# Eight gate blocks in seven-product pairs, and the SSD output product beside attention, on one core of Trainium2

## The chip, the cores and the metric

The kernel runs on one core of one Trainium2 chip. The metric is the device time of one execution in microseconds (us), from the median of several runs; lower is better.

## The reference

One decoder block on a sequence of 1024 tokens and 1024 channels, all in float32. Cut to what matters here:

```python
h = rms_norm(x, pre_norm1_w) * (1.0 + sc1) + sh1
proj = h @ w_in
z, xbc, dt_raw, q, k, v, gates = split(proj)
y_ssd = ssd_branch(z, xbc, dt_raw, ...)                 # (1024, 1024), before its output product
y_att = diff_attention_branch(q, k, v, ...)             # 8 heads, each with two softmaxes
gate_ssd, gate_att = split(sigmoid(gates), 2)           # 1024 channels each
merged = gate_ssd * (y_ssd @ w_ssd_o) + gate_att * (y_att @ w_attn_o)
mix = merged @ w_out
x = x + g1 * rms_norm(mix, post_norm1_w)
# then a gated conv-FFN on x
```

## The kernel before

**Products.** Each float32 product is made of three matmuls, with both sides split into a high and a low part (`split`: ACT copies the high part, DVE subtracts to get the low part). A "block" is 128 output channels by all 1024 tokens. It needs 8 slices of the contraction, two halves of 512 tokens and three matmuls each: 48 matmuls of 128x512. Two blocks can also be made as a pair in seven products instead of eight (Strassen's scheme in Winograd's form, on halves of the contraction and of the tokens): 84 matmuls instead of 96, with extra sums of weights on DVE and extra sums of results on ACT and DVE. The sums of the token side (`HX`) are made once and serve all pairs.

**Order of the stages.** After the first norm:

1. Four SSD gate blocks (0 to 3) as plain blocks; the first is begun with the norm.
2. The loop over `pairs`: SSD gate blocks 4 to 7, one q/k pair, ten convolution blocks. While pair m runs, `post` finishes pair m-1. In the second and third pair the first sums of `w_ada` (`ada_sum`) run too.
3. The z, dt and v products and the SSD recurrence by chunks. At its end y lies in DRAM (`yd`), tokens by channels.
4. The q/k blocks 0 and 1: the list `seq` names the blocks in order, `fetch_seq` loads a block's weights two blocks ahead, `split_seq` splits them one block ahead. Between the halves of a block, `turn_y` turns columns of y: TensorE transposes four 128x128 pieces of `yr` (loaded from `yd`, one token half at a time by `load_y`), ACT and DVE make the high and the low part in `yT`, which stays in SBUF. The result of a q/k block gets its rotation in `rope` (ACT copy to `qf`, DVE `stream_shuffle` to `sw`, POOL and DVE products, a DVE sum, then `split` into `thhi`, `thlo`), and `store_qk` sends it to DRAM in 16 DMAs of 64 KB, high and low parts in turn.
5. The SSD output product: eight blocks of `w_ssd_o` on `yT`, each multiplied by its gate (`gsd`, DVE) and stored in `msd`.
6. Attention, head by head, eight blocks of 128 queries each. Its scores, transposes and value products leave TensorE waiting for softmax, so plain blocks fill in: `dense_stream` is a generator that gives three matmuls per step, and `fill(n)` takes n steps. It runs 18 blocks: q/k blocks 3 to 7 and the eight attention gate blocks `ga`. Work for ACT and DVE beside it (splits of weights, low parts, norms) stands in the queue `bg`, from which `run_bg` takes steps. `load_heads` loads q and k (`qst`, `kst`, `klo`) and v (`vt`) of the next head; the q and k of head 0 are loaded during stage 5.
7. The attention output product, merged with `msd` and the attention gate `gad`, and the rest of the layer.

**Order on the engines.** In stages 2 to 5 TensorE, DVE, ACT and SP (the queue that issues the DMAs) follow the program's order. In stage 6 TensorE, DVE, ACT and POOL do, and SP is ordered by the scheduler. SBUF is cut into 43 slots of 4 KB per partition (`SL`), given out first in, first out. `ps_wa` gives two PSUM banks in turn, `ps_wb` and `ps_wc` one each.

## Time and profile before

| | |
|---|---|
| Median of 3 runs | 1892.37 us (1890.81 to 1895.33) |
| Span of the profiled execution | 1889.7 us |
| TensorE busy | 1859.7 us, 98% |
| VectorE (DVE) busy | 1298.1 us, 69% |
| ScalarE (ACT) busy | 882.8 us, 47% |
| GpSimd (POOL) busy | 146.1 us, 8% |
| Mean granted TensorE clock | 0.994 |
| DMA | 322.09 MB, 170 GB/s over the span |

The profiled execution's own time is its span, which runs from the first to the last instruction. Lines of the trace have the source line, the engine, the result and the operands by the program's names, the number of instructions (x) and their times. "Idle before, <- releaser" is the time that the engine stood before an instruction, and what it waited for.

### The profile page before, as it was taken

What the parts mean: (1) busy time and instruction counts of PE and PEld (TensorE: products, weight loads), DVE (VectorE), ACT (ScalarE), POOL (GpSimd) and SP (SyncE); (2) the same over time, 40 slices, a digit from 0 to 9 for tenths busy, and PEclk for the clock granted to TensorE, in tenths of its full rate; (3) what the DMA queues carried; (4) which work ended last, traced back from release to release, by engine and by line L of the source; (5) the groups of instructions that cost most, each with busy time, mean ns of one, the idle gap of its engine ahead of it and who ended that gap; (6) DMA issues with size and microseconds to landing.
All of it is one profiled execution on the core that took longest, in us unless ns stands there. A gap on an engine that the chain in (4) does not pass through costs nothing.

```text
span 1889.7 us, 24926 instructions
## 1 busy us (share of the span) xinstructions
PE 1859.7 (98%) x9224; PEld 1561.0 (83%) x9224; DVE 1298.1 (69%) x1983; ACT 882.8 (47%) x1715; POOL 146.1 (8%) x139
## 2 busy tenths in 40 slices
PE   8999999999999999999999999999999999999998
PEld 8888889987888888888888788887878888888886
DVE  3677777689755237767667465377888888876545
ACT  4543542355543126565656323465554545465532
POOL 0000000045522000000000010000000000000001
PEclk8999999999999999999999999999999999999999
DMA  7447256678737746666542756022333322368744
GB/s 283 136 149 250 95 172 210 210 253 311 258 125 175 230 165 164 164 194 167 159 135 97 238 201 218 39 85 99 113 106 111 106 101 95 117 222 306 249 150 159
DMA packets 131898, 322.09 MB, mean 170 GB/s; under 512 B 17216, under 2 KB 41152, under 8 KB 131776
## 3 DMA queue, kind: packets, MB, share of 16 engines
q1 hardware_dynamic: 130464, 317.30, 51.5%
q0 software_dynamic: 1312, 3.19, 0.5%
q8 instruction: 73, 1.20, 0.3%
q14 instruction: 49, 0.40, 0.1%
HBM read 225.26 MB, written 95.17 MB: 170 GB/s over the span
## 4 chain that ended last, share of the span: by engine, by line
PE 82%; DVE 8%; ACT 4%; DMA 3%; issue 2%; SPq 0%; POOL 0%; POOLq 0%; ACTq 0%; DVEq 0%
PE upx L1772 3%; PE upx L1771 3%; PE upx L1773 3%; PE o L1463 3%; PE dx L2135 2%; PE dx L2136 2%; PE dx L2134 2%; PE dy L2136 2%; PE dy L2134 2%; PE dy L2135 2%; PE z L117 2%; PE z L118 2%; PE so L116 2%; PE ao L118 2%; PE ao L117 2%
## 5 line engine op out<-in xcount | busy, mean ns | idle before, releaser
L1771 PE MATMUL upx<-t,wu_t 128*128 128x512 f32 x264 | 103.6, 392 | 2.3 <-ACT evs L2191 1.6
L1772 PE MATMUL upx<-t,wu_t 128*128 128x512 f32 x264 | 103.0, 390 | 0.2 <-DVE t L1889 0.2
L1773 PE MATMUL upx<-t,wu_t 128*128 128x512 f32 x264 | 102.9, 390 | 0.0
L1745 ACT ACTIVATE wu_t<-sab 128x512 fp32r<-128x512 f32 x57 | 34.1, 627 | 129.8 <-DVE sab L1762 129.8
L1451 ACT COPY aT<-at 128x512 f32<-128x512 f32 (+2 forms) x96 | 46.1, 480 | 103.1 <-PE at L1450 103.1
L1463 PEld LDWEIGHTS o<-vt,aT 128*128 128x128 f32 x576 | 74.6, 191 | 9.8 <-ACT aT L1451 5.8
L95 DVE TENSOR_TENSOR g_lo<-gst,g_hi 128x1024 fp32r<-128x1024 f32 (+1 forms) x42 | 47.5, 1135 | 49.8 <-ACT g_hi L94 49.7
L1463 PE MATMUL o<-vt,aT 128*128 128x128 f32 x576 | 81.0, 277 | 0.3
L94 ACT ACTIVATE g_hi<-gst 128x1024 fp32r<-128x1024 f32 (+1 forms) x42 | 41.3, 987 | 64.7 <-DMA gst<-gld_s 35.7
L1424 DVE TENSOR_REDUCE nmx<-sc 128x1 f32<-128x640 f32 (+3 forms) x64 | 65.6, 1024 | 2.2
L1404 PE MATMUL sc<-kst,qst 128*128 128x512 f32 (+2 forms) x192 | 63.9, 341 | 0.0
L1405 PE MATMUL sc<-klo,qst 128*128 128x512 f32 (+2 forms) x192 | 63.2, 346 | 0.0
L1771 PEld LDWEIGHTS upx<-t,wu_t 128*128 128x128 f32 x264 | 49.6, 188 | 14.6 <-ACT evs L2191 2.0
L1789 DVE SCALAR_TENSOR_TENSOR ug<-cg,vec,ug 128x1023 f32<-128x1023 f32 (+1 forms) x44 | 56.3, 1280 | 6.8 <-ACT ug L1788 5.9
L1772 PEld LDWEIGHTS upx<-t,wu_t 128*128 128x128 f32 x264 | 49.6, 188 | 10.6 <-DVE t L1889 0.5
L1773 PEld LDWEIGHTS upx<-t,wu_t 128*128 128x128 f32 x264 | 49.6, 188 | 10.3
L1749 DVE TENSOR_TENSOR wu_t<-sab,wu_t 128x512 fp32r<-128x512 f32 x57 | 39.3, 690 | 26.5 <-ACT wu_t L1745 26.5
L1789 DVE SCALAR_TENSOR_TENSOR uv<-cv,vec,uv 128x1023 f32<-128x1023 f32 (+1 forms) x44 | 56.2, 1278 | 0.9 <-ACT uv L1788 0.9
L1440 DVE RECIPROCAL rsm<-ssum 128x2 f32<-128x2 f32 x64 | 10.6, 165 | 63.9 <-ACT p L1437 36.4
L1450 PE MATMUL at<-ident,p 128*128 128x128 f32 x288 | 47.8, 275 | 6.7 <-DVE p L1442 5.2
L143 POOL TENSOR_TENSOR rsf<-rsf,nhalf 128x1 f32<-128x1 f32 x8 | 5.6, 703 | 627.8 <-DVE rsf L142 625.1
L1442 DVE SCALAR_TENSOR_TENSOR p<-p,coef,p 128x128 f32<-128x128 f32 (+3 forms) x64 | 52.4, 818 | 2.2
(536 smaller groups left out, 5994.4 us busy)
## 6 DMA issues: line engine op xcount, KB each, us to landing
adas<-in_w_ada SPq DMA_DIRECT2D x32, 512.0 KB, 4.9
wdr<-in_w_down SPq DMA_DIRECT2D x22, 512.0 KB, 6.3
wtd<-wds SPq DMA_DIRECT2D x22, 512.0 KB, 4.8
wuf<-in_w_up SPq DMA_DIRECT2D x22, 512.0 KB, 3.5
gld_s<-gsum SPq DMA_DIRECT2D x22, 512.0 KB, 2.8
gst<-gld_s SPq DMA_DIRECT2D x20, 512.0 KB, 4.4
wdt_raw<-wtd SPq DMA_DIRECT2D x20, 512.0 KB, 4.9
wuv<-in_w_up SPq DMA_DIRECT2D x19, 512.0 KB, 3.5
```

Source lines behind the costliest of these rows:

```text
L117: T.matmul(ps, lh, rl, start=False, stop=False)
L118: T.matmul(ps, ll, rh, start=False, stop=(i == n - 1))
L1404: T.matmul(sc[:, n0:n1], qs_[s][:, tsl], ks_[s][:, n0:n1], start=True, stop=False)
L1424: V.reduce_max(nmx[:, bq, s : s + 1], sc[:, :L], axis=AX.X, negate=True)
L1463: T.matmul(po_of[j, grp][:, qi, :], at[:, k, :], vt[j % 2][:, kt, :], start=(kt == 0), stop=(kt == i))
L1771: T.matmul(out_, wh, xh_, start=(k == 0 and first), stop=False, skip_group_check=not first)
L1772: T.matmul(out_, wh, xl_, start=False, stop=False, skip_group_check=not first)
L1773: T.matmul(out_, wl, xh_, start=False, stop=(k == end), skip_group_check=not first)
L1789: V.scalar_tensor_tensor(u[:, d:], c_[:, : S - d], fw[:, 2 - d : 3 - d], u[:, d:], op0=ALU.mult, op1=ALU.add)
L2134: T.matmul(o, gh[:, kk, tsl], wh, start=(k == 0 and not more), stop=False, skip_group_check=more)
L2135: T.matmul(o, gh[:, kk, tsl], wl, start=False, stop=False, skip_group_check=more)
L2136: T.matmul(o, gl[:, kk, tsl], wh, start=False, stop=(k == KF - 1), skip_group_check=more)
```

## The change

The eight attention gate blocks leave attention and become four more pairs in the loop of stage 2. The SSD output product takes their place among the blocks that fill attention. Since y's columns would need sixteen slots until then, `turn_y` stores each in DRAM (`ytd`, 0.5 MB per column and token half), and each half is loaded back into the slots of `hT` as soon as the last q/k block has used that half; the last two q/k blocks and the first two SSD blocks are ordered by halves for this. The gate product of the SSD blocks goes to POOL (two operations per half, after a copy from PSUM by ACT). Stage 5 is gone. The weights of the first two attention blocks (`w_q3`, `w_k3`) are the fifth and sixth in `seq`; the rotation of the block `w_k` 1 becomes background work at the start of attention, ahead of the other steps in `bg`; head 0's q and k are loaded at the end of the third block of stage 4.

```diff
-    pairs = [("gs", 4, 5), ("gs", 6, 7), ("qk", 2, 2)] + [("xbc", b, b + 1) for b in range(2, 12, 2)]
+    pairs = [("gs", b, b + 1) for b in range(4, 16, 2)] + [("qk", 2, 2)] + [("xbc", b, b + 1) for b in range(2, 12, 2)]
...
-                SP.dma_start(gsd[b], c_)
+                SP.dma_start((gsd + gad)[b], c_)
...
-    seq = [("w_q", 0), ("w_k", 0), ("w_q", 1), ("w_k", 1)] + [("w_ssd_o", j) for j in range(8)]
+    seq = [("w_q", 0), ("w_k", 0), ("w_q", 1), ("w_k", 1), ("w_q", 3), ("w_k", 3)]
...
     def turn_y(k, half):
-        yT[k][half] = new_hl(f"yT{k}_{half}")
+        y_ = new_hl(f"yt{k}_{half}")
...
+        A.activation(y_[:, 0, :], ps, AF.Copy, scale=nw)
+        V.scalar_tensor_tensor(y_[:, 1, :], ps, nw, y_[:, 0, :].bitcast(F32), op0=ALU.mult, op1=ALU.subtract)
+        SP.dma_start(ytd[k][half], y_.bitcast(F32))
+        SL.put(y_)
...
+    def rope_steps(kind, b, ps):
+        return [
+            lambda: A.activation(qf, ps.rearrange("p h t -> p (h t)"), AF.Copy, scale=qscale[kind]),
+            lambda: (V.stream_shuffle(sw, qf, perm), G.tensor_tensor(qf, qf, ropc, op=ALU.mult)),
+            lambda: V.tensor_tensor(sw, sw, rops, op=ALU.mult),
+            lambda: V.tensor_tensor(qf, qf, sw, op=ALU.add),
+            lambda: split(th_hi, th_lo, qf),
+        ]
...
+            if n == 2:
+                qst, kst, klo = [[[SL.get(f"{x_}0_{s}", F32R) for s in range(2)]] for x_ in ("qst", "kst", "klo")]
+                for s in range(2):
+                    load_qk(s, qst[0][s], kst[0][s], klo[0][s])
...
-        for j in range(8):
...
-            block_half(ps[:, 0, :], seq_w[j + 4], yT, 0)
...
-                V.scalar_tensor_tensor(mout[:, hsl], gth[:, hsl], 1.0, ps[:, half, :], op0=ALU.add, op1=ALU.mult)
...
-    blocks = [(kind, b) for b in (3, 4, 5) for kind in ("w_q", "w_k")] + [("ga", 0)]
-    blocks += [(kind, b) for b in (6, 7) for kind in ("w_q", "w_k")] + [("ga", g) for g in range(1, 8)]
+    NQK = 10
+    blocks = [(kind, b) for b in range(3, 8) for kind in ("w_q", "w_k")] + [("so", j) for j in range(8)]
+    units = []
+    for n in range(len(blocks)):
+        units += [(n, 0), (n, 1)] if n not in (8, 9, 10, 11) else [(n // 2 * 2, n % 2), (n // 2 * 2 + 1, n % 2)]
...
+    def load_yT(half):
+        for k in range(KD):
+            SL.put(hT[k][half])
+            yT[k][half] = SL.get_last(f"yT{k}_{half}", F32R, (P, 2, HALF))
+            SP.dma_start(yT[k][half].bitcast(F32), ytd[k][half])
...
     def dense_stream():
-        fetch(0)
-        fetch(1)
-        split_later(0)
...
+        raws[1] = seq_w[5]
+        splits[0] = seq_w[4]
+        finished.add(("w", 0))
+        for u, (n, half) in enumerate(units):
...
+            if kind == "so":
+                g_, m_ = [t[:, u % 2, :] for t in gate_io]
+                A.activation(m_, ps, AF.Copy)
+                G.tensor_tensor(g_, g_, m_, op=ALU.mult)
+                G.tensor_tensor(m_, m_, g_, op=ALU.add)
+                SP.dma_start(msd[j][:, hsl], m_)
+                if u + 2 < len(units):
+                    gate_in(u + 2)
...
+            if n == NQK - 1:
+                load_yT(half)
...
+    later("rope", *rope_steps(*old)[:4], lambda: (split(th_hi, th_lo, qf), store_qk(*old[:2], th_hi, th_lo)))
     with tc.manual_schedule(engines={EN.PE, EN.DVE, EN.Activation, EN.Pool}):
-        for _ in range(NFIRST - 6):
+        for n in range(NFIRST - 6):
             fill(1)
-            run_bg(2)
+            run_bg(2 if n % 2 else 1)
```

In the new program SP's order around this point is: the stores of y's columns 5, 6 and 7 of the first half; the loads of `yr` for the second half; the store of `w_q` 0; `w_q3`; most of head 0's `vt`; two columns of y; the store of `w_k` 0; three columns of y; head 0's q and k (ten DMAs); `w_k3`; three columns of y; the store of `w_q` 1; then the store of `w_k` 1.

More of the change, by code (lines that the diff above doesn't have):

```diff
@@ L394 @@
     kld = [dp.tile([64, S], F32, tag=f"kld{m}", name=f"kld{m}") for m in range(NH)]
+    ytd = [[dp.tile([P, 2, HALF], F32, tag=f"ytd{k}_{h}", name=f"ytd{k}_{h}") for h in range(2)] for k in range(KD)]
     rowd = [dp.tile([1, D], F32, tag=f"rowd{i}", name=f"rowd{i}") for i in range(4)]
@@ L1201 @@
     SL.put(vev)
-    yT = [[None] * 2 for _ in range(KD)]
     n_turn = 0
     def turn_y(k, half):
-        yT[k][half] = new_hl(f"yT{k}_{half}")
+        y_ = new_hl(f"yt{k}_{half}")
         nonlocal n_turn
@@ L1214, in turn_y @@
         nw = vec[:, V_SN + k : V_SN + k + 1]
-        A.activation(yT[k][half][:, 0, :], ps, AF.Copy, scale=nw)
-        V.scalar_tensor_tensor(yT[k][half][:, 1, :], ps, nw, yT[k][half][:, 0, :].bitcast(F32), op0=ALU.mult, op1=ALU.subtract)
-    hi, lo = [SL.get(f"th{n}", F32R) for n in ("hi", "lo")]
+        A.activation(y_[:, 0, :], ps, AF.Copy, scale=nw)
+        V.scalar_tensor_tensor(y_[:, 1, :], ps, nw, y_[:, 0, :].bitcast(F32), op0=ALU.mult, op1=ALU.subtract)
+        SP.dma_start(ytd[k][half], y_.bitcast(F32))
+        SL.put(y_)
+    th_hi, th_lo = [SL.get(f"th{n}", F32R) for n in ("hi", "lo")]
     qf = SL.get("qf")
@@ L1226, in split_seq, with rope @@
             split(*seq_w[n], raw)
-    def rope(kind, b, ps):
-        A.activation(qf, ps.rearrange("p h t -> p (h t)"), AF.Copy, scale=qscale[kind])
-        V.stream_shuffle(sw, qf, perm)
-        G.tensor_tensor(qf, qf, ropc, op=ALU.mult)
-        V.tensor_tensor(sw, sw, rops, op=ALU.mult)
-        V.tensor_tensor(qf, qf, sw, op=ALU.add)
-        split(hi, lo, qf)
+    def rope_steps(kind, b, ps):
[6 more added lines that the diff above has]
+        ]
+    def rope(*block):
+        for f_ in rope_steps(*block):
+            f_()
     turns = [((0, 1), (2, 3, 4)), ((5, 6, 7), ())] * 2
@@ L1254 @@
                 if half == 0 and old is not None:
-                    store_qk(*old[:2], hi, lo)
+                    store_qk(*old[:2], th_hi, th_lo)
+            if n == 2:
+                qst, kst, klo = [[[SL.get(f"{x_}0_{s}", F32R) for s in range(2)]] for x_ in ("qst", "kst", "klo")]
+                for s in range(2):
+                    load_qk(s, qst[0][s], kst[0][s], klo[0][s])
             old = (*seq[n], ps)
         SL.put(*yr)
-        gths = [SL.get(f"gth{i}") for i in range(2)]
-        mouts = [SL.get(f"mout{i}") for i in range(2)]
-        SP.dma_start(gths[0], gsd[0])
-        for j in range(8):
-            gth, mout = gths[j % 2], mouts[j % 2]
-            fetch_seq(j + 6)
-            if j + 1 < 8:
-                SP.dma_start(gths[(j + 1) % 2], gsd[j + 1])
-            ps = ps_mm(f"so{j}")
-            block_half(ps[:, 0, :], seq_w[j + 4], yT, 0)
-            if j == 0:
-                rope(*old)
-                store_qk(*old[:2], hi, lo)
-                SL.put(hi, lo, ropc, rops, qf, sw)
-                qst, kst, klo = [[[SL.get(f"{n}0_{s}", F32R) for s in range(2)]] for n in ("qst", "kst", "klo")]
-            split_seq(j + 5)
-            block_half(ps[:, 1, :], seq_w[j + 4], yT, 1)
-            for half in range(2):
-                hsl = slice(half * HALF, (half + 1) * HALF)
-                V.scalar_tensor_tensor(mout[:, hsl], gth[:, hsl], 1.0, ps[:, half, :], op0=ALU.add, op1=ALU.mult)
-            if j in (3, 4):
-                s = j - 3
-                load_qk(s, qst[0][s], kst[0][s], klo[0][s])
-            SP.dma_start(msd[j], mout)
-    SL.put(*gths, *mouts)
-    for k in range(KD):
-        SL.put(*yT[k])
     vt = [SL.get(f"vt{i}", F32, (P, 8, P)) for i in range(2)]
-    for t, n in ((qst, "qst"), (kst, "kst"), (klo, "klo")):
-        t.append([SL.get(f"{n}1_{s}", F32R) for s in range(2)])
     thl = [[SL.get(f"tq{n}{i}", F32R) for n in ("hi", "lo")] for i in range(2)]
@@ L1295 @@
     osb = SL.get("osb", F32, (P, 2, 4, P))
-    gev = SL.get("gev", F32, (P, 2, HALF))
     ssum = const("ssum", [P, 2, 2])
@@ L1303 @@
     sqt = const("sqt", [P, 4])
-    blocks = [(kind, b) for b in (3, 4, 5) for kind in ("w_q", "w_k")] + [("ga", 0)]
-    blocks += [(kind, b) for b in (6, 7) for kind in ("w_q", "w_k")] + [("ga", g) for g in range(1, 8)]
+    NQK = 10
[3 more added lines that the diff above has]
+        units += [(n, 0), (n, 1)] if n not in (8, 9, 10, 11) else [(n // 2 * 2, n % 2), (n // 2 * 2 + 1, n % 2)]
     emitted = {"scores": 0, "values": 0}
-    raws, splits = {}, {}
+    raws, splits, begun = {}, {}, set()
     finished.clear()
@@ L1316, in fetch @@
             raws[n] = wp.tile([P, KD, P], F32, tag="wraw", name=f"{kind}{j}_raw", bufs=3)
-            SP.dma_start(raws[n].rearrange("p k c -> p (k c)"), a["w_gate"][8 + j] if kind == "ga" else a[kind][j])
+            SP.dma_start(raws[n].rearrange("p k c -> p (k c)"), a["w_ssd_o" if kind == "so" else kind][j])
     def split_later(n):
@@ L1343, in low_part @@
         bg.appendleft((("low", kind, b, half), f_))
-    def dense_stream():
-        fetch(0)
-        fetch(1)
-        split_later(0)
-        for n, (kind, j) in enumerate(blocks):
-            fetch(n + 2)
-            need(("w", n))
-            split_later(n + 1)
-            w = splits.pop(n)
-            for half in range(2):
-                ps = ps_wa(f"{kind}p{j}_{half}")
-                for k in range(KD):
-                    xh_, xl_ = hT[k][half][:, 0, :], hT[k][half][:, 1, :]
-                    T.matmul(ps, w[0][:, k, :], xh_, start=(k == 0), stop=False)
-                    T.matmul(ps, w[0][:, k, :], xl_, start=False, stop=False)
-                    T.matmul(ps, w[1][:, k, :], xh_, start=False, stop=(k == KD - 1))
-                    if k < KD - 1:
-                        yield
-                hsl = slice(half * HALF, (half + 1) * HALF)
-                if kind == "ga":
-                    A.activation(gev[:, half, :], ps, AF.Tanh, scale=0.5)
-                    SP.dma_start(gad[j][:, hsl], gev[:, half, :])
-                else:
-                    hi, lo = thl[n % 2]
-                    A.activation(hi[:, hsl], ps, AF.Copy, scale=qscale[kind])
-                    low_part(kind, j, half, ps, hi, lo)
-                yield
@@ new lines, with gate_in @@
+    yT = [[None] * 2 for _ in range(KD)]
+    gate_io = []
+    def load_yT(half):
[3 more added lines that the diff above has]
+            SP.dma_start(yT[k][half].bitcast(F32), ytd[k][half])
+    def gate_in(u):
+        n, half = units[u]
+        SP.dma_start(gate_io[0][:, u % 2, :], gsd[blocks[n][1]][:, half * HALF : (half + 1) * HALF])
+    def dense_stream():
+        raws[1] = seq_w[5]
+        splits[0] = seq_w[4]
+        finished.add(("w", 0))
+        for u, (n, half) in enumerate(units):
+            kind, j = blocks[n]
+            if u == 2 * NQK:
+                for kind_ in ("w_q", "w_k"):
+                    need(("low", kind_, 7, 1))
+                SL.put(*thl[0], *thl[1])
+                gate_io.extend(SL.get(n_, F32, (P, 2, HALF)) for n_ in ("gin", "gout"))
+                gate_in(u)
+                gate_in(u + 1)
+            if n not in begun:
+                begun.add(n)
+                fetch(n + 2)
+                need(("w", n))
+                split_later(n + 1)
+            w = splits[n]
+            src = yT if kind == "so" else hT
+            ps = ps_wa(f"{kind}p{j}_{half}")
+            for k in range(KD):
+                xh_, xl_ = src[k][half][:, 0, :], src[k][half][:, 1, :]
+                T.matmul(ps, w[0][:, k, :], xh_, start=(k == 0), stop=False)
+                T.matmul(ps, w[0][:, k, :], xl_, start=False, stop=False)
+                T.matmul(ps, w[1][:, k, :], xh_, start=False, stop=(k == KD - 1))
+                if k < KD - 1:
+                    yield
+            hsl = slice(half * HALF, (half + 1) * HALF)
+            if kind == "so":
[6 more added lines that the diff above has]
+                    gate_in(u + 2)
+            else:
+                hi, lo = thl[n % 2]
+                A.activation(hi[:, hsl], ps, AF.Copy, scale=qscale[kind])
+                low_part(kind, j, half, ps, hi, lo)
+            if n == NQK - 1:
+                load_yT(half)
+            yield
@@ L1378, in load_heads @@
         assert emitted["scores"] >= 8 * (j - 1) and emitted["values"] >= 8 * (j - 1)
+        if j == 1:
+            SL.put(th_hi, th_lo, ropc, rops, qf, sw)
+            for t, n in ((qst, "qst"), (kst, "kst"), (klo, "klo")):
+                t.append([SL.get(f"{n}1_{s}", F32R) for s in range(2)])
         if j > 0:
@@ L1576 @@
             if t == 55:
-                SL.put(*thl[0], *thl[1], *qst[0], *kst[0], *klo[0], vt[0])
+                SL.put(*qst[0], *kst[0], *klo[0], vt[0])
                 stg = [SL.get(f"stg{i}", F32, (P, 2, HALF)) for i in range(2)]
@@ L1582 @@
                 for _ in range(2 if i % 2 else 1):
-                    if n_att < 10:
+                    if n_att < 9:
                         att_split()
@@ L1599 @@
             run_bg(1)
-            if n % 2 == 1 and n < 9:
+            if n % 2 == 1 and n < 11:
                 att_split()
@@ L1605 @@
         assert n_att == len(parts)
-        SL.put(osb, gev, *stg)
+        SL.put(osb, *stg, *gate_io)
         for k in range(KD):
-            SL.put(*hT[k])
+            SL.put(*yT[k])
         mT = [[None] * 2 for _ in range(KD)]
```

## The prediction

> **What bounds the kernel now.** I read the page first, then the busy time by stage, then what each engine waits for, then the timelines of SP, ACT, DVE and PE around 541 to 605 us.

> ```profile
> span 1889.7 us, 24926 instructions
> PE 1859.7 (98%) x9224; PEld 1561.0 (83%) x9224; DVE 1298.1 (69%) x1983; ACT 882.8 (47%) x1715; POOL 146.1 (8%) x139
> ```

> TensorE is busy nearly throughout, so a matmul that goes is worth its time, and a wait of TensorE that comes is lost. Busy time by stage (length, PE, PEld, DVE, ACT, POOL, granted clock, DMA share, GB/s):

> ```profile
> 134.00:153.50 19.50, 19.50 (x88) 16.15 (x87) 15.51 (x20) 8.20 (x14) 0.00 (x0) 1.00 0.82 273
> 173.00:268.20 95.20, 95.20 (x422) 78.88 (x421) 77.45 (x98) 50.60 (x75) 1.17 (x2) 1.00 0.40 128
> 541.80:592.90 51.10, 51.07 (x258) 42.81 (x257) 29.89 (x36) 20.37 (x30) 11.32 (x5) 1.00 0.45 123
> 592.90:680.10 87.20, 87.20 (x387) 72.24 (x386) 25.93 (x33) 11.71 (x13) 3.43 (x1) 1.00 0.75 227
> 680.10:1065.50 385.40, 377.92 (x2177) 321.40 (x2176) 260.21 (x535) 221.78 (x594) 16.52 (x16) 1.00 0.56 159
> ```

> The rows are: the second pair in seven products, the last five pairs, the four q/k blocks with the turning of y, the SSD output product, and attention. The SSD output product has DVE at 26 of 87 us: it is a stage in which SP, ACT and DVE can finish late work at no cost. It is what the change removes.

> **The gain.** Eight blocks go from 592.9 to 680.1:

> ```profile
> L116 PE MATMUL so<-yT,w_ssd_o_hi x128: 388/389/390, 593.0 to 679.4; 128*128 128x512 f32 x128
> L118 PE MATMUL so<-yT,w_ssd_o_lo x128: 388/389/390, 593.5 to 679.9; 128*128 128x512 f32 x128
> ```

> That is 384 matmuls in 87.2 us, 0.227 us each. Attention keeps its number of filling matmuls (864: ten q/k blocks and eight others, before and after). Four more pairs come at 95.20 / 5 = 19.04 us each (84 x 0.227 gives 19.07), 76.2 in all, so the gain is 87.2 - 76.2 = 11.0 us. If the new pairs ran like the one at 134 us it would be 1.8 less, but that one lies beside the w_ada sums, which keep their places. I take 11.0.

> **The cost.** The y columns are now stored on SP, a queue that issues in order. The program also gives every DMA one of eight counters in turn, and an issue waits until the DMA eight places ahead has landed. Before:

> ```profile
> 561.77 1.74 SPq L1119 DMA_DIRECT2D yr<-yd  x4
> 567.52 0.42 SPq L418 DMA_DIRECT2D qd<-thlo  x1
> 569.58 0.30 SPq L417 DMA_DIRECT2D qd<-thhi  x1
> 570.87 0.30 SPq L418 DMA_DIRECT2D qd<-thlo  x1
> 573.54 0.42 SPq L418 DMA_DIRECT2D qd<-thlo  x1
> 574.00 0.42 SPq L417 DMA_DIRECT2D qd<-thhi  x1
> 572.85 1.03 PE L1213 MATMUL ytr<-ident,yr 128*128 128x128 f32 x8
> 566.73 2.06 DVE L1216 SCALAR_TENSOR_TENSOR yT<-ytr,vec,yT 128x512 fp32r<-128x512 f32 x3
> 576.08 1.06 ACT L94 ACTIVATE thhi<-qf 128x1024 fp32r<-128x1024 f32 x1 [7.45 <-DMA qd<-thhi]
> 578.32 1.22 DVE L95 TENSOR_TENSOR w_k_lo<-w_k_raw,w_k_hi 128x1024 fp32r<-128x1024 f32 x1
> 580.66 0.48 PE L116 MATMUL w_kp<-hT,w_k_hi 128*128 128x512 f32 x1
> ```

> The holes ahead of 569.58 and 570.87 are the seventh and eighth piece of the q store waiting for the third and fourth load of yr. So yr's second half landed by 570.8, 9.1 us after its first issue, 2 us ahead of the transposes at 572.85. Pieces follow each other by 0.46 us, and one has landed 2.1 us after its issue (574.00 to 576.08, where ACT may overwrite thhi). All times below are on this clock.

> *First hole.* After the change the stores of columns 5 to 7 stand ahead of yr on SP. They need DVE's results, the last at 566.73 + 2.06 = 568.8. yr starts at 569.3 instead of 561.8, behind 1.57 MB of y. The best stretches move 361 GB/s, those with the loads of k 231:

> ```profile
> 631.00:633.00 2.00, 2.00 (x11) 1.65 (x10) 0.00 (x0) 0.77 (x1) 0.00 (x0) 1.00 0.99 361
> 635.00:637.00 2.00, 2.00 (x10) 1.67 (x9) 0.24 (x1) 0.00 (x0) 0.00 (x0) 1.00 1.01 231
> ```

> 1.57 MB is 4.4 us, of which 1.8 pass before 569.3. With 0 to 2.6 added to 569.3 + 9.1, yr lands between 578.4 and 581; I take 579.5. PE loses 6.6 us at the transposes.

> *Second.* Pieces 5 to 8 of the q store wait for one yr load each, seven more take 3.2 us, and the last high piece has landed at 584.9, not 576.08. ACT's next thhi waits for it, and behind it on ACT are the weights of the fourth block and the y columns. From thhi's start to the end of w_k_lo are 3.46 us (576.08 to 579.54): 588.4. The next y column on DVE (0.69) ends at 589.1, and only then has the third transpose of that group its PSUM bank (two are in turn). The fourth block starts at 589.3 instead of 580.66: 8.7 lost in all.

> *Third.* The k store waits behind the second y column (589.8), its fifteenth piece goes at 596.6 and lands at 598.7. There thhi of the third block starts, and 3.46 later w_q3's low half is ready, 602.2. PE, ready at 592.9 + 8.7 = 601.6, starts attention's first block about then (its third matmul is the first to need it): 9.0 lost.

> *Fourth, the largest.* Next on SP, from 597.6, are three y columns, ten loads of q and k for head 0, w_k3 and three y columns: 6.8 MB. Only then comes the q store of the third block. At 0.36 MB/us the bytes take 18.9 us, with the 2.1 MB of k at 0.23 22.2; I take 20.5 and 1.5 to start. The last lands at 619.6; seven pieces (3.2) and a landing (2.1) later, at 625, the store is over. If only issuing counted (17 at 0.5, 14 at 0.46, 2.1) it would be 614.6; at the slow rate with a late start 627.5. [...]

> The rope of w_k1 is now background work on ACT, ahead of the weights of attention's second block (w_k3). Its thhi waits for that store, and ACT works in order.

> ```profile
> L95 DVE TENSOR_TENSOR thlo<-qf,thhi x4: 1226/1226/1226, 564.5 to 601.5; 128x1024 fp32r<-128x1024 f32 x4
> L1332 ACT ACTIVATE w_k_hi<-w_k_raw x10: 617/630/655, 669.1 to 878.7; 128x512 fp32r<-128x512 f32 x10
> L1329 DVE TENSOR_TENSOR w_k_lo<-w_k_raw,w_k_hi x10: 680/683/685, 671.2 to 882.2; 128x512 fp32r<-128x512 f32 x10
> L1339 DVE SCALAR_TENSOR_TENSOR tqlo<-w_qp,tqhi 128x512 fp32r<-128x512 f32 x10 | 6.9, 688 | 9.3 <-ACT tqhi L1369 8.7 <-DMA klo<-kld 0.7
> L1358 PE MATMUL w_kp<-hT,w_k_hi x60: 388/476/487, 691.4 to 915.9; 128*128 128x512 f32 x60
> ```

> After 625 come thhi 1.06, thlo 1.23, two low halves 1.37 (the high halves lie beside thlo) and tqlo 0.69, which frees the bank: 629.3. Without loss PE would be there at 592.9 + (691.4 - 680.1) = 604.2. So 25.1 us are lost in all (the 9.0 included); 614.6 makes it 14.7, 627.5 makes it 27.6. Nothing fills it: the work behind is on PE, in order.

> *Attention itself.* 8.4 MB of y come back in two halves of 4.2 MB, 11.7 us at 0.36, each beside 16 filling steps of 385.4 / 288 = 1.34 us, 21.4; the loads of a head (3.1 MB) share one of them. It is hidden, with little to spare. Tanh becomes a copy of the same size, and the gate goes to POOL, 32 operations:

> ```profile
> L1037 POOL TENSOR_TENSOR xdd<-xd,sm x14: 1042/1456/2021, 375.8 to 507.4; 128x512 f32<-128x512 f32 x14
> PE at L1450 <- DVE p L1442: 5.2, 14, 1.2
> ```

> 32 x 1.46 = 47 us of POOL over 170 us; it is late for nobody but attention's norm, whose power DVE waits for. TensorE's wait for DVE in attention is 5.2 us now. A gain is excluded, since its cause stays; doubled it is +5. I take +2 for both, 0 to +5.

> *Sum.* -11.0 + 25.1 + 2 = +16.1 on the profiled span of 1889.7: 1905.8. The median of the runs, 1892.37, lies 2.7 above that span: 1908.5, call it 1908. By the bounds: -11.0 + 14.7 = +3.7 to -9.2 + 27.6 + 5 = +23.4, that is 1896 to 1916.

> **Rivals.**
> *Faster: the queue recovers.* If TensorE's loss at attention's second block stays under 11 us, the change gains; that needs the q store of the third block landed by about 611. For it: DVE and ACT have room, and in the profile yr was 2 us early. Against it: even pure issue gives 614.6. With the first hole alone, -11.0 + 6.6 and nothing after: 1888; with part of the y stores slipping through, 1884.
> *y comes back late.* Head 5's loads and the second half of y collide, and the SSD product stands until the last column is in: one half more, 11.7 us, 1920. For it: both are queued on SP within 25 us. Against: 42.8 us for both halves.
> *The port.* If POOL's operations held DVE up, each by half its length, 32 x 0.73 = 23 us, all on PE's path: 1930 (1908 less the 2 already there). Against it:

> ```profile
> L1233 DVE TENSOR_TENSOR sw<-sw,rops x4: 1224/1226/1226, 558.6 to 595.6; 128x1024 f32<-128x1024 f32 x4
> L1232 POOL TENSOR_TENSOR qf<-qf,ropc x4: 3354/3424/3434, 558.7 to 595.7; 128x1024 f32<-128x1024 f32 x4
> ```

> Starting together, DVE kept its 1.22 us and POOL took more than twice its shortest half-size operation. [...]

> That the change doesn't do what it says is excluded: the built program has 48 matmuls fewer.

> **How the numbers follow.** Forecast 0.64, faster 0.18, late y 0.13, port 0.05. About 0.2% (3.8 us) can be told from no change. Faster takes 0.16 of the rival's 0.18; 0.05 for the same holds its rest and the low edge of the forecast; slower 0.79. The forecast's own range is 1896 to 1916; with the upper part of the faster rival (1888) and the lower part of late y it is 1887 to 1918.

> **What would show it.** Right: ytr waits 5 to 8 us for yr; thhi waits for DMA three times, the last over 10 us; the largest TensorE wait is at attention's second block (w_kp after w_k_lo or tqlo), about 15 us; the pairs stay at 19.0 us. Wrong: yr lands before 574, or the q store of the third block lands before 611, or the waits lie at the SSD product's first columns instead.

## The result, and the profile after

| | before | after |
|---|---|---|
| Median of the runs | 1893.7 us (1890.81 to 1895.33) | 1948.01 us (1941.73 to 1950.35) |
| Span of the profiled execution | 1889.7 us | 1945.7 us |
| Mean granted TensorE clock | 0.994 | 0.981 |
| DMA | 322.09 MB | 338.86 MB |

The ratio is 1.0279, 95% interval 1.0265 to 1.0293: 54 us slower, where 14 to 16 were forecast. The page of after, first its totals:

```profile
span 1945.7 us, 24999 instructions
PE 1863.1 (96%) x9176; PEld 1560.5 (80%) x9176; DVE 1326.5 (68%) x2014; ACT 907.5 (47%) x1758; POOL 192.0 (10%) x171
```

There are 48 matmuls fewer, but TensorE's busy time is 3.4 us longer. Something made matmuls slow, besides the waits. Busy time by stage (columns as in the prediction: length, PE, PEld, DVE, ACT, POOL, granted clock, DMA share, GB/s): five of the twelve pairs, the four q/k blocks with the turning of y, and attention.

```profile
173.00:268.40 95.40, 95.40 (x421) 79.00 (x422) 50.96 (x76) 40.18 (x65) 0.00 (x0) 1.00 0.36 122
621.80:682.30 60.50, 53.85 (x258) 44.19 (x257) 27.38 (x34) 18.84 (x28) 11.37 (x5) 0.94 0.64 208
682.30:1120.50 438.20, 386.08 (x2178) 325.22 (x2177) 280.27 (x545) 226.86 (x601) 63.22 (x47) 0.96 0.65 187
```

Five pairs take 95.4 us, 19.1 each, so the gain of 11 us is there. The q/k blocks take 60.5 instead of 51.1 us and attention 438.2 instead of 385.4: 62 us more. TensorE's waits in the q/k blocks and at the start of attention, where w_qp and w_kp are its first and second filling block and sc the scores of head 0 (start, duration, instruction, in brackets the idle time before it and what ended it):

```profile
655.68 0.30 PE L1212 MATMUL ytr<-ident,yr 128*128 128x128 f32 x1 [2.63 <-DMA yr<-yd]
660.29 1.33 PE L1212 MATMUL ytr<-ident,yr 128*128 128x128 f32 x5 [0.80 <-DMA yr<-yd]
684.31 0.50 PE L1364 MATMUL w_qp<-hT,w_q_lo 128*128 128x512 f32 x1 [1.30 <-DVE w_q_lo L95]
697.94 0.40 PE L1419 MATMUL sc<-kst,qst 128*128 128x128 f32 x1 [4.09 <-DMA kst<-khd]
700.00 0.45 PE L1420 MATMUL sc<-klo,qst 128*128 128x128 f32 x1 [1.67 <-DMA klo<-kld]
714.14 0.80 PE L1362 MATMUL w_kp<-hT,w_k_hi 128*128 128x512 f32 x1 [11.03 <-DVE tqlo L1320]
```

And ACT's, in the same view:

```profile
665.44 1.06 ACT L94 ACTIVATE thhi<-qf 128x1024 fp32r<-128x1024 f32 x1 [16.77 <-DMA qd<-thhi]
680.21 1.06 ACT L94 ACTIVATE thhi<-qf 128x1024 fp32r<-128x1024 f32 x1 [8.30 <-DMA khd<-thhi]
709.97 1.06 ACT L94 ACTIVATE thhi<-qf 128x1024 fp32r<-128x1024 f32 x1 [25.11 <-DMA qd<-thhi]
```

The waits for yr, ACT's three and the one at w_kp are the four steps of the prediction, 80.0 us later on this clock; TensorE's wait of 5.8 us for head 0's kst and klo is not among them. The largest wait of TensorE, however, is another one that the prediction does not have. SP, ACT and TensorE where the SSD blocks begin in attention:

```profile
925.03 8.90 SPq L1398 DMA_DIRECT2D vt<-vd  x8
934.04 4.26 SPq L1333 DMA_DIRECT2D yT<-ytd  x8
939.01 0.32 SPq L421 DMA_DIRECT2D khd<-tqhi  x1
945.36 0.30 SPq L422 DMA_DIRECT2D kld<-tqlo  x1
947.00 1.62 SPq L1337 DMA_DIRECT2D gin<-gsd  x2
948.66 0.91 SPq L1298 DMA_DIRECT2D so_raw<-in_w_ssd_o  x2
954.88 1.15 ACT L1313 ACTIVATE so_hi<-so_raw 128x512 fp32r<-128x512 f32 x2 [15.27 <-DMA so_raw<-in_w_ssd_o]
956.65 1.12 PE L1465 MATMUL at<-ident,p 128*128 128x128 f32 x4 [14.90 <-ACT osb L1511]
```

The eight loads of y's second half take all eight counters. Everything issued behind them waits (the next eight issues stand 7.5 us in all for these loads), and the last thing there, at 948.66, is the weights of the third SSD block. ACT stands for them 15.27 us, in order; behind it on ACT is the operation (L1511) that empties the PSUM bank in which TensorE's next transposes go. TensorE stood for no column of y. And after each of these stops it came back at half clock (length, PE busy, granted clock, DMA share, GB/s):

```profile
697.00:702.00 5.00, 2.40 (x6) 0.60 1.02 348
702.00:707.00 5.00, 1.12 (x3) 0.50 0.69 204
707.00:712.00 5.00, 0.00 (x0) 0.50 0.74 182
712.00:717.00 5.00, 2.85 (x7) 0.50 0.65 133
717.00:722.00 5.00, 5.00 (x24) 0.85 0.83 172
942.00:947.00 5.00, 0.00 (x0) 0.68 1.02 371
947.00:952.00 5.00, 0.00 (x0) 0.50 0.93 319
957.00:962.00 5.00, 5.00 (x23) 0.62 0.97 290
962.00:967.00 5.00, 5.00 (x31) 1.00 1.00 215
```

Busy time times what is missing of the clock is 1.0 + 0.6 us in the first two rows, after the stop at head 0's scores, 1.4 + 0.8 us in the rows from 712, after the stop at w_kp, and 1.9 us in the row from 957. After the waits for yr it is some 2 us more (clock 0.70 and 0.61 in the two windows from 655 to 665 us).

### The profile page after: what moved, and what is told of

Same layout as the page of the kernel before. It is cut to its first block, busy times and chain, and to the rows that moved or that the text cites. A ratio compares the mean times of both kernels' runs of the same rounds, so it can differ in the third digit from the quotient of the medians.

```text
span 1945.7 us, 24999 instructions
## 1 busy us (share of the span) xinstructions
PE 1863.1 (96%) x9176; PEld 1560.5 (80%) x9176; DVE 1326.5 (68%) x2014; ACT 907.5 (47%) x1758; POOL 192.0 (10%) x171
## 2 busy tenths in 40 slices
DMA packets 137658, 338.86 MB, mean 174 GB/s; under 512 B 17856, under 2 KB 41792, under 8 KB 137536
## 3 DMA queue, kind: packets, MB, share of 16 engines
q0 software_dynamic: 1312, 3.19, 0.4%
## 4 chain that ended last, share of the span: by engine, by line
PE 72%; DVE 11%; DMA 7%; ACT 5%; issue 3%; SPq 2%; POOL 0%; POOLq 0%; DVEq 0%; ACTq 0%
PE upx L1787 3%; PE upx L1788 3%; PE upx L1789 3%; PE o L1478 2%; PE xx L493 2%; PE xx L494 2%; PE xx L495 2%; PE dx L2151 1%; PE ao L117 1%; PE ao L116 1%; PE ao L118 1%; PE dx L2152 1%; PE upy L1787 1%; PE upy L1788 1%; PE dx L2150 1%
## 5 line engine op out<-in xcount | busy, mean ns | idle before, releaser
L95 DVE TENSOR_TENSOR g_lo<-gst,g_hi 128x1024 fp32r<-128x1024 f32 (+1 forms) x42 | 47.5, 1134 | 50.6 <-ACT g_hi L94 50.5
L1465 PE MATMUL at<-ident,p 128*128 128x128 f32 x288 | 48.7, 279 | 26.3 <-ACT osb L1511 14.9
L94 ACT ACTIVATE g_hi<-gst 128x1024 fp32r<-128x1024 f32 (+1 forms) x42 | 41.4, 988 | 65.1 <-DMA gst<-gld_s 37.3
L1465 PEld LDWEIGHTS at<-ident,p 128*128 128x128 f32 x288 | 34.9, 142 | 37.0 <-ACT osb L1511 15.0
L493 PE MATMUL xx<-xt,xw_t 128*128 128x512 f32 x144 | 56.1, 390 | 1.5 <-DVE xcv L700 1.5
```

The costliest lines, as they stand in the source:

```text
L95: V.tensor_tensor(lo, raw, hi.bitcast(F32), op=ALU.subtract)
L493: T.matmul(o, wh, xh_, start=(k == 0 and first), stop=False, skip_group_check=not first)
L1465: T.transpose(ptr[:, k * P : (k + 1) * P], pt_[i % 2][0][:, (k0 + k) * P : (k0 + k + 1) * P], ident)
```

## The experiments

Ratios are against the kernel before, timed beside each run on the same chip (its medians there lie between 1894.3 and 1895.0 us). The clock of the first 60 us differs between executions (see the end: in two traces the z product began 5.4 us apart); stretches of the trace are compared from the z product on.

**1. Without the way through memory.** Three kernels: `no_y` drops the stores and the loads (the SSD product multiplies `hT` in y's place), `no_yback` only the loads, `no_ystore` only the stores (the loads read the gates' buffer).

```diff
-        SP.dma_start(ytd[k][half], y_.bitcast(F32))                       # no_y, no_ystore
...
-            SP.dma_start(yT[k][half].bitcast(F32), ytd[k][half])
+            yT[k][half] = hT[k][half]                                     # no_y, no_yback
+            SP.dma_start(yT[k][half].rearrange("p h t -> p (h t)").bitcast(F32), gsd[k])   # no_ystore
```

> Leaves out both trips of y: turn_y does not store the columns, and the SSD output product in attention runs on hT in y's place (same matmuls, no loads of y). Theory 1, the y transfers hold up the SP queue: nearly all of the loss goes; what is left is head 0's loads and the rotation at the border of attention, about 7 us, against the gain of 11, so 1890 to 1898 us. Theory 2, the SSD product in attention costs by itself (no slack stage left, gate product on POOL): most of the loss stays, over 1925 us.

> Stores y but never loads it back: the SSD output product in attention runs on hT. Theory 1: the stop at the first SSD blocks (0 to 4 of them, some 17 us and the half clock after it) goes, the start of attention stays as it is: 1922 to 1931 us. Theory 2: 1940 us or more.

> Leaves out the stores of y's columns; the loads in attention stay, of the same size, but read the gates' buffer. Theory 1: the waits for yr go, and the wait at attention's second block shrinks from 11 us to under 5, the stop at the SSD blocks stays: 1908 to 1920 us. Theory 2: 1940 us or more.

Measured: `no_y` 1905.65 us (ratio 1.0060, 1.0045 to 1.0075), `no_yback` 1932.15 (1.0188, 1.0161 to 1.0214), `no_ystore` 1926.47 (1.0163, 1.0139 to 1.0188). So the loads cost 16 us, the stores 21.5, both 42. The stop of 14.9 us at the SSD blocks is gone in `no_yback` and remains (13.9) in `no_ystore`. All three stayed above what the first theory gave: `no_yback` by 1 us, `no_ystore` by 6.5, with 6.2 us left at w_kp where under 5 were expected, and `no_y` by 8. `no_y` is still 22 us above the 1883 that 1894 less the gain would give.

**2. The pairs alone.** The eight gates as pairs; the SSD product stays a stage of its own, and attention keeps its pace until its ten q/k blocks run out.

```diff
-    pairs = [("gs", 4, 5), ("gs", 6, 7), ("qk", 2, 2)] + ...
+    pairs = [("gs", b, b + 1) for b in range(4, 16, 2)] + [("qk", 2, 2)] + ...
...
-    blocks += [(kind, b) for b in (6, 7) for kind in ("w_q", "w_k")] + [("ga", g) for g in range(1, 8)]
+    blocks += [(kind, b) for b in (6, 7) for kind in ("w_q", "w_k")]
```

> The kernel before with only the first half of the change: the attention gates are made as four more pairs, the SSD output product stays a stage of its own ahead of attention, and attention fills with the ten q/k blocks alone, at the same pace, so that its second half has no filling. If filling matters little: 76 us more in pairs, 87 us less in attention, 1883 us. If each of the 28 unfilled items stands 1 to 2 us longer on softmax than its own matmuls: 1910 to 1940 us. The pairs themselves stay at 19.0 to 19.2 us each in both cases.

Measured: 1955.49 us (ratio 1.0323, 1.0302 to 1.0344), beyond both expectations. Attention without filling:

```profile
971.00:1141.00 170.00, 119.23 (x650) 95.98 (x650) 108.57 (x225) 90.06 (x246) 8.82 (x8) 0.90 0.44 131
```

TensorE stands 51 of 170 us and works at a clock of 0.90. Blocks that leave attention leave its softmax uncovered, so something else has to fill it; the full change, with the SSD product there, is 7 us faster than this. `pairs_dense` keeps the SSD product as a stage ahead of attention, and in its trace TensorE waits neither at head 0's scores nor at attention's second block.

**3. Order on SP, or bytes?** The same stores of y, issued by POOL.

```diff
-        SP.dma_start(ytd[k][half], y_.bitcast(F32))
+        G.dma_start(ytd[k][half], y_.bitcast(F32))
```

> The sixteen stores of y go out on POOL's queue instead of SP's, with the same bytes at the same places. Theory 1 (what costs is the order on SP, where each issue stands behind the DMA eight places ahead of it): about what leaving the stores out gave, 1948 to 1920-1932 us, and the third-to-first step's waits for yr (6.1 us) go. Theory 2 (what costs is the 8 MB on the sixteen DMA engines, whoever issues them): 1943 us or more, with the waits for yr and for the q stores where they were.

Measured: 1932.78 us (1.0205, 1.0190 to 1.0221). Of the 21.5 us, 15 come back with the same bytes when the stores leave SP's queue. The waits for yr are gone, and w_kp still waits 9.5 us. In the profile these stores also lie in another DMA queue (its traffic rises from 3.19 to 11.58 MB), so the order of issue on SP and the order within a DMA queue are not told apart here.

**4. The third SSD block's weights ahead of y.** Only one fetch moves.

```diff
-                fetch(n + 2)
+                if n != NQK:
+                    fetch(n + 2)
...
             if n == NQK - 1:
+                if half == 0:
+                    fetch(n + 3)
                 load_yT(half)
```

> The full change, with one fetch moved: the weights of the third SSD block are fetched ahead of the first half of y instead of behind the second. Theory 1 (the stop of 14.9 us among the SSD blocks is the order on SP: so_raw behind y and the q stores): the stop and the half clock behind it go, 1948 to 1930-1937 us. Rival (y's own 8 MB, or the weights after these, are late instead): 1943 or more, with TensorE waiting at the SSD blocks for yT, the gates or the next weights.

Measured: 1933.61 us (1.0208, 1.0189 to 1.0226), 14.4 less. TensorE's 14.9 us at L1465 are gone. Of the 16 us that the loads cost, nearly all was this one load that stood behind them. A smaller stop has come up a little later: the store of attention's result (`atd`) stands behind y as well, ACT waits 5.4 us for it before it may write the next one, and TensorE 4.6 us behind ACT.

**5. The rotation of w_k 1 later.** Four of its operations behind the split of w_k 3, its own split and stores after attention's third item.

```diff
-    later("rope", *rope_steps(*old)[:4], lambda: (split(th_hi, th_lo, qf), store_qk(*old[:2], th_hi, th_lo)))
...
+            if n == 0:
+                later(None, *rope_steps(*old)[:4])
...
+            if t == 2:
+                split(th_hi, th_lo, qf)
+                store_qk(*old[:2], th_hi, th_lo)
```

> Only the rotation of the block w_k 1 is placed otherwise: its first four operations behind the split of w_k 3, its own split and its stores after the third item of attention. Theory 1 (ACT stands in order at thhi until the q block's stores are over, and w_k 3's split stands behind it: 11.0 us at w_kp, then 10 us of TensorE at half clock, which are worth about 5 more): 1948 to 1930-1938 us, and no long wait of w_kp for tqlo. Rival (the data are late whoever waits for them, and the stop moves to the scores of head 0 or of head 1): 1943 us or more.

Measured: 1946.45 us (1.0278, 1.0263 to 1.0294), the rival's result. The waits of ACT and of TensorE (in all, times, longest):

```profile
ACT w_k_hi L1313 <- DMA w_k_raw<-in_w_k: 18.3, 1, 18.3
PE sc L1419 <- DMA kst<-khd: 9.0, 2, 4.5
PE w_kp L1362 <- DVE tqlo L1320: 6.5, 1, 6.5
PE sc L1420 <- DMA klo<-kld: 5.6, 4, 1.9
```

With the rotation out of the way, ACT stands 18.3 us for the weights of w_k 3 themselves. They were late on SP too, and the wait at thhi had hidden that.

**6. So the weights earlier, and head 0's loads behind the third block's stores** (with the stores of y on POOL's queue).

```diff
-            fetch_seq(n + 2)
+            if n < 3:
+                fetch_seq(n + 2)
+            if n == 2:
+                fetch_seq(5)
...                                  # load_qk of head 0: from the end of n == 2 to behind store_qk at n == 3
```

> On top of y's stores on POOL's queue (1932.8 us): the weights of w_k 3 are fetched a block earlier, ahead of head 0's loads, and head 0's loads stand behind the stores of the third block instead of ahead of them. The rotation of w_k 1 stays first in attention. Theory 1 (order on SP): the q stores are over some 8 us sooner, ACT's wait at thhi before attention (18.3 us) and TensorE's 9.5 us at w_kp with some 5 us of half clock behind it go: 1916-1923 us. Rival (the sixteen DMA engines are full here, at a share of 0.9 to 1.0 from 640 to 690 us, so that another order only names another one late): 1929 or more, with the stop at head 0's first scores (kst, klo) instead.

Measured: 1936.05 us (1.0223, 1.0204 to 1.0241), no better than 1932.78. The wait of w_kp for tqlo is gone, and in its place stands this:

```profile
PE sc L1422 <- DMA kst<-khd: 8.1, 2, 4.8
PE sc L1423 <- DMA klo<-kld: 4.9, 3, 1.8
```

**7. POOL's gate product.** On the kernel without y's traffic, and side by side with it over more runs:

```diff
-                A.activation(m_, ps, AF.Copy)
-                G.tensor_tensor(g_, g_, m_, op=ALU.mult)
-                G.tensor_tensor(m_, m_, g_, op=ALU.add)
+                V.scalar_tensor_tensor(m_, g_, 1.0, ps, op0=ALU.add, op1=ALU.mult)
```

> The kernel without y's stores and loads (the SSD product runs on hT in place of y), with the gate product in one DVE operation from PSUM, as before, instead of a copy on ACT and two products on POOL. Theory of the port (DVE stands while POOL works: its oT subtraction took 846 ns instead of 688, its one-column coef 324 instead of 220, beside POOL's 16 products; TensorE's waits at the transposes for p 10.1 us against 5.2): the 1905.6 us of its base fall to 1896-1901. Rival (DVE, which carries 0.9 us more in each of 16 halves, is as late with p as before): 1904-1912.

> The kernel without y's stores and loads, POOL's gate products in it, beside the same with the gate on DVE: the two were timed alike (1905.65 and 1905.4 us), though the stretch from the first scores to the attention output product took 403.3 us in one trace and 393.7 in the other. Theory of the port: the 9.6 us are real and were covered by the granted clock of the first 60 us, which is drawn anew in each run (0.74 against 0.67 from 20 to 40 us; the stage after it began 5.5 us apart): over more runs this kernel is 4-9 us above the other, 1904-1909. Rival: the two are level, within 2 us, and the traces differ by chance.

> The same with the gate product in one DVE operation. Theory of the port: 1897-1902 us, the stretch from the first scores to the output product again 8-10 us shorter than with POOL's products. Rival: within 2 us of the other kernel.

Measured: 1905.4 us the first time, level with `no_y`; side by side 1902.61 (1.0039, 1.0023 to 1.0054) against 1906.81 (1.0070, 1.0054 to 1.0086). From the first scores to the attention output product the traces have 403.3 against 393.7 us, and 398.9 against 394.8. So POOL's products cost about 4 us, with the first pair of traces at up to 10. The two intervals just touch, and the stretch of the second pair is 4.1 us shorter where 8 to 10 were expected. TensorE's wait for p, with POOL's products and without:

```profile
PE at L1462 <- DVE p L1454: 10.1, 16, 1.4
PE at L1460 <- DVE p L1452: 4.8, 11, 0.9
```

With POOL's products some DVE operations take longer: from 900 us on, oT's subtraction has a mean of 847 ns in `no_y_again` and 687 in `no_y_dve_again` (688 in the kernel before), the one-column coef 328 and 220 (220), a 128x256 sum of p 1214 and 486 (485). Not all do: a 128x512 sum of p has 752 in `no_y_again` and 751 before. The edit also takes sixteen copies off ACT, so what of the 4 us is DVE's lateness alone was not measured.

**8. The repairs together.** `repair`: y's stores and loads on POOL's queue, the rotation late, the gate on DVE. `repair2`: experiments 3 and 4 and the gate on DVE. `repair3`: experiments 3 and 4 only. `repair4`: `repair2`, with the first gate pieces loaded ahead of y as well.

```diff
-                gate_io.extend(...)          # repair4: at the start of the SSD blocks
-                gate_in(u)
-                gate_in(u + 1)
...
                 if half == 0:
+                    gate_io.extend(...)      # ahead of load_yT(0)
+                    gate_in(2 * NQK)
+                    gate_in(2 * NQK + 1)
                     fetch(n + 3)
```

> All together on the full change, y stored and loaded: y's stores and its loads both on POOL's queue, the rotation of w_k 1 late as above, the gate product on DVE. Theory 1 (the losses are orders on queues and on engines, each of its own): 1948 less about 21 (stores), 14 (rotation and clock), 15 (loads, with the weights of w_ssd_o no longer behind them) and 5 (port), 1885-1900 us. Rival (the 16 MB are in the way whoever issues them, and the stops move): 1910 or more.

> On the full change, three edits that each touch another loss: y's stores on POOL's queue (alone -15.2 us), the third SSD block's weights fetched ahead of y (alone -14.4), the gate product on DVE. If the losses are separate: 1948 less 15, 14 and 5 to 9, 1909-1915 us, with the stop before attention (w_kp for tqlo, 9.5 us) the largest that is left. If they cover one another: 1920 or more.

> The full change with two edits: y's stores on POOL's queue and the third SSD block's weights ahead of y; the gate product stays on POOL. If these two losses are separate: 1948 less 15 and 14, 1916-1922 us, and no stop at the SSD blocks. If the burst of y only changes its victim: 1926 or more.

> As repair3, with the gate product on DVE and the first two gate pieces loaded ahead of y too (in repair2 DVE stood 16.9 us for them behind the second half of y, and TensorE 18.8 us at so_lo behind DVE). Theory (the burst of y stops whatever is queued behind it and is needed at once; with nothing of that kind behind it, no stop is left): 3 to 6 us under repair3, 1911-1918 us, with w_kp for tqlo (about 9.5 us) as the longest wait of TensorE. Rival: another stop of 5 us or more at the SSD blocks, 1922 or more.

Measured: `repair` 1922.58 us (1.0153, 1.0127 to 1.0178), `repair2` 1927.1 (1.0169, 1.0155 to 1.0184), `repair3` 1923.27 (1.0149, 1.0134 to 1.0164), `repair4` 1917.7 (1.0108, 1.0084 to 1.0132). The two edits of `repair3` together give 25 us of the 30 that they give apart. `repair` missed its expectation most and lies with its rival. With y's stores and loads on POOL's queue, SP's eight loads of vt took 12.68 us to issue, where the full change took 8.90, and the weights behind them were late again:

```profile
908.93 12.68 SPq L1396 DMA_DIRECT2D vt<-vd  x8
PE sop L1364 <- DVE so_lo L1310: 9.2, 1, 9.2
```

`repair2` missed by a stop that had come back elsewhere:

```profile
PE sop L1365 <- DVE so_lo L1310: 18.8, 1, 18.8
943.38 0.69 DVE L1371 SCALAR_TENSOR_TENSOR gout<-gin,sop 128x512 f32<-128x512 f32 x1 [16.86 <-DMA gin<-gsd]
```

The gate pieces stand behind y too. While POOL did the product, only POOL waited for them (23.9 us in the full change); on DVE, in order, they held the split of the next weights. With these loads ahead of y as well, `repair4` has the expected time, and TensorE's longest wait is w_kp for tqlo, 9.5 us. But that no stop would be left was wrong. The store of attention's result stands behind the second half of y, as in experiment 4:

```profile
945.15 0.69 SPq L1513 DMA_DIRECT2D atd<-osb  x1
950.79 0.31 ACT L1494 ACTIVATE osb<-osb 128x128 f32<-128x128 f32 x1 [6.38 <-DMA atd<-osb]
952.38 1.22 PE L1479 MATMUL o<-vt,aT 128*128 128x128 f32 x4 [5.48 <-ACT aT L1467]
```

So the burst of y held up three things in turn that were not y: the weights, the gate pieces and the store.

**9. No turned y in memory at all.** y stays in `yd`, where the recurrence left it. It is loaded two columns at a time, and turned in attention straight into the slots of `hT`, one group per item; the gate is on DVE. `turn_late` has head 0's loads as in experiment 6, `turn_late2` where the change has them; both fetch the weights of w_k 3 early, as there.

```diff
+        for q in range(4):
+            SP.dma_start(yg[g % 2][:, q, :], yd[4 * half + q][:, c * 2 * P : (c + 1) * 2 * P])
...
             run_bg(1)
+            turn_group()
             values(t, 0, *x[0])
```

> y is not turned before attention at all: it stays in yd, where the recurrence left it, and is loaded (4 MB, in pieces of two columns) and turned two columns per item when the last q/k block has used the half, straight into hT's slots. No stores and loads of turned y (16 MB less), the gate product on DVE, and the order on SP of the run before the last. Theory (the change lost by y's way through memory, the SP order at the border and POOL's products, in that order): 1886-1898 us, about level with before. Rival (attention cannot take the SSD product and the turns beside the softmax): 1905 or more, with waits of TensorE for p, aT or yT among the SSD blocks.

> y turned in attention as in the run before (1912.0 us), with head 0's loads back where the change had them, at the end of the third block of stage 4, so that they stand ahead of the stores of the third block and have those in front of them less. Order theory: head 0's scores no longer wait (10.2 us for kst and klo, and the half clock after it), 1897-1904 us. Rival (DMA capacity): the wait is taken over by thhi behind the third block's stores, as in the full change, 1909 or more. In neither case is it below before: the turns themselves leave TensorE some 11 us idle from 870 to 940 us.

Measured: 1912.0 us (1.0093, 1.0077 to 1.0109) and 1910.68 (1.0087, 1.0071 to 1.0103). The border moved its wait again: 10.2 us of scores for kst and klo in the first, 7.6 of w_kp for tqlo in the second, the rival's way. From 870 to 940 us, where the columns are turned, TensorE is busy 59.96 of 70 us; in `no_y_dve_again` 67.20. No version of the change reached the kernel before.

## Why the prediction was right or wrong

The profiled execution took 1945.7 us where the sum gave 1905.8: 39.9 us more. Of these, 30 lie in "attention itself", 5 in the fourth step, and the rest is spread over stages that the sum took as unchanged (2.0 of it ahead of the pairs).

**The gain** was right: 19.1 us a pair.

**First, second and third step** were right in cause and size. yr landed at 660.2 (580.2 on the clock before, forecast 579.5) and TensorE lost 6.1 us for it (6.6); thhi began at 585.4 (584.9), the next at 600.2 (598.7).

**Fourth step: right in place, past its upper bound in size, wrong as to the one cause.** thhi began at 630.0, forecast 625, bounds 614.6 to 627.5; w_kp at 634.1 against 629.3, 29.9 us lost instead of 25.1. The 5 us are in the queue of this step, which began 1.4 us later and took 25.6 us instead of 22.0 until the last y column let the eighth piece out:

```profile
679.04 2.48 SPq L1216 DMA_DIRECT2D ytd<-yt  x3
704.68 0.30 SPq L419 DMA_DIRECT2D qd<-thlo  x1
```

The step put the loss on ACT's order alone, and some of the 29.9 us were spent elsewhere, 5.8 of them at head 0's scores. Experiments 5 and 6 showed three late things close behind one another: the q store, the weights of w_k 3, head 0's loads. Whichever was taken out, the next one stood nearly as long. A part of it stays without the stores and loads of turned y: `no_y_dve_again` and `turn_late2` still wait 6.5 and 7.6 us at w_kp, while before and `pairs_dense`, which have the SSD product as a stage, wait neither there nor for kst. So the removed stage of 87 us (by this comparison of kernels; no run moves the cover alone), called in the prediction a stage in which late work finishes at no cost, had been the cover for the way of q and k through memory; the prediction priced y's stores against it and not the loss of that cover.

**The clock after a stop: no term.** Busy PE time at a lowered clock is worth 1.6 us after head 0's scores, 2.2 after the stop at w_kp and 1.9 after the one at the SSD blocks.

**"Attention itself", +2, 0 to +5: this step failed.** From w_kp's start to the attention output product the change took 406.5 us, before 374.2: 32.3 more, of which 26.5 are waits of TensorE and 5.7 slower matmuls. The one wait that the step priced, for p, rose from 5.2 to 9.9 us, near its bound of +5. The rest had no term, above all the 14.9 us at the SSD blocks. "It is hidden, with little to spare" asked whether y comes back in time for its columns; it did. What stands behind it on the same queue was not asked, and that was the third SSD block's weights: 14.4 us (experiment 4). The rival of a late y named the place and nearly the price, 11.7 us, but a cause that did not occur; that its price came near is luck.

**The rival called the port** (POOL's operations hold DVE up) stood at 23 us with a chance of 0.05. The runs show times, not a port. Taking POOL's products out gave about 4 us (experiment 7). In the prediction's two rows, which start together, DVE kept its 1.22 us; in rows of after a one-column DVE operation took 1.03 us beside POOL's product and 0.22 us without one:

```profile
1001.28 1.29 POOL L1371 TENSOR_TENSOR gin<-gin,gout 128x512 f32<-128x512 f32 x1 [7.04 <-ACT gout L1370]
1002.65 1.28 POOL L1372 TENSOR_TENSOR gout<-gout,gin 128x512 f32<-128x512 f32 x1
1002.91 1.03 DVE L1456 SCALAR_TENSOR_TENSOR coef<-ssum,nlam,rsm 128x1 f32<-128x1 f32 x1
1009.44 0.22 DVE L1456 SCALAR_TENSOR_TENSOR coef<-ssum,nlam,rsm 128x1 f32<-128x1 f32 x1
```

POOL began first, at 1002.65, and ended at 1003.93; DVE's one-column operation began at 1002.91 and ended at 1003.94.

**The account.** In medians, with its rounding: 1883 by the products alone; 19 to 20 for the border and attention without y's traffic (`no_y_dve_again`, 1902.6, of which waits at w_kp, w_k_lo, vt, so_lo and klo are 6.5, 2.2, 1.9, 1.8 and 1.5); 4 for POOL; 41 for y's stores and loads, of which some 15 and 14 came back when the order on one queue was changed. The five waits come to 13.9 us. Busy PE time at a lowered clock, in windows of 5 us from 671 to 1075 us of the same trace, is worth a further 5 us, so that some 19 of the 19 to 20 us are named.

## What to carry to other kernels

A stage in which TensorE is busy and the other engines are idle is cover for whatever was started before it: when it goes, price every queue that used it, not only the work that is added. Of a burst of loads ask not only whether its own data come in time but what is issued behind it on that queue, and which engine would stand for it in order. Where several things are late at one place, moving the one that the profile names may only uncover the next.

## What the runs showed of the hardware

*The clock of the first 60 us differs between executions.* The windows from 0 and from 20 us of `no_y_again` and then of `no_y_dve` (length, PE busy, granted clock, DMA share, GB/s), with the same program up to there:

```profile
0.00:20.00 20.00, 18.94 (x154) 1.00 0.89 325
20.00:40.00 20.00, 15.87 (x75) 0.74 0.85 319
```

```profile
0.00:20.00 20.00, 18.94 (x132) 0.88 0.89 333
20.00:40.00 20.00, 15.88 (x70) 0.67 0.75 282
```

Busy time times what is missing of the clock is 4.1 us in the first and 7.5 in the second, with 1.2 more from 40 to 60 us (0.94). The z product began at 342.2 us in the first and at 347.6 in the second, a difference of 0.3% of the span. In the first pair of traces of experiment 7 the z product began at 342.1 and 347.6 us, which hides 5.5 of the 9.6 us in those two executions. How much of the spread of all runs it makes was not measured.
